# The output gate of the recurrence loaded into the slot of the squares, ahead of the variance sums

## The chip, the core and the metric

The kernel runs on one core of one Trainium2 chip. A core has five engines with an instruction queue each: TensorE (PE, with its weight loads shown as PEld), VectorE (DVE), ScalarE (ACT), GpSimd (POOL) and SyncE (SP). An engine works through its own queue in order and waits at an instruction whose operands or whose memory slot is not free yet. Most DMA transfers are issued from SP's queue, some from POOL's. The metric is the device time of one execution in microseconds (us); the median of three runs is given.

## The reference

The reference is one block of a network: two token mixers side by side (a softmax attention with forgetting, "fox", and a linear recurrence, "rwkv7"), and a feed-forward part behind them. The sequence has 1024 tokens, the model 1024 columns, each mixer 8 heads of 64. The change touches only the end of the recurrence, the normalisation of each head's output and the output gate:

```python
_, y = lax.scan(step, state0, (...))
mean = jnp.mean(y, axis=-1, keepdims=True)
var = jnp.mean(jnp.square(y - mean), axis=-1, keepdims=True)
y = ((y - mean) * lax.rsqrt(var + GN_EPS)).reshape(bsz, seq, RWKV_WIDTH) * ln_w + ln_b
bonus = (jnp.sum(r_h * k_h * r_k, axis=-1, keepdims=True) * v_h).reshape(bsz, seq, RWKV_WIDTH)
return ((y + bonus) * g).astype(p.dtype)
```

Here g is the output gate, `sigmoid(xg) @ g2`, which does not depend on the recurrence.

## The kernel before, in words

The kernel is one program in stages: modulation and normalisation of the input; low-rank products for decay, learning rate and output gate, written to a DRAM tensor d_lora; the recurrence; the attention heads; the output projections; the feed-forward part.

The recurrence works on transposed data: 128 rows are two heads of 64, 512 columns are half of the sequence. That gives eight units, p = 0..3 (pairs of heads) times hf = 0, 1 (halves of the sequence), in this order. Each unit is a coroutine `pre` (preparation: cumulative decay sums cum at L715, exponentials el and en at L719 and L721, the products of the chunks, and the inverse of a triangular matrix by steps on DVE, L784 and L786, with tiles E, t and M) and a coroutine `main` (the copies X and TT of the inverse at L852 and L859, products uw and mz, the chain of states S at L903, and the end of the unit). `pre` of the next unit runs beside `main` of this one. Between their steps PE gets matmuls of the big projections, which need no recurrence: queries and keys (qk), the recurrence's own inputs (ps_rkv), values (v) and gates (gt). A small planner, class Weave, writes this mixture by estimated times. It fixes PE's order. The order of DVE, ACT, POOL and SP in this stage is laid out by the framework when the program is built: by the planned readiness of each instruction, so a change of one wait can move its neighbours.

The end of a unit, L914 to L938, works on tiles of 128x512 in slots of one buffer each, named by their tag. y is the recurrence's output. `head_sums` (L690) adds up each head's 64 rows with a matmul against a block matrix blk_r, in two parts, high and low: ACT casts the high part (L692), POOL subtracts to get the low part (L693), and PE multiplies both. The first call gives the mean (tile mu), which is subtracted at L923. The squares ysq (L925, slot "ysq") go through head_sums a second time, with the parts in the slots "Zt" and "Wt", and give the variance va. rs is the norm factor, exp(-0.5 ln(var + eps)), by two ACT steps (L930, L931), in the slot "ysq". Two DVE steps (L932, L933) scale y and add the bias and the bonus. The gate gg is loaded by SP (L935) into the slot "Zt", the product o is made at L937 in the slot "ysq", and stored to DRAM (L938).

Two neighbours matter at the eighth unit's end. Gate projections run beside it: a half of 24 matmuls goes to one of two PSUM buffers ("big"), ACT takes three steps (L337 to L339) in an SBUF tile gs, DVE one (L340), which reads the PSUM buffer last, ACT one more (L341), and SP stores it (L342, d_gate<-gs). gs has two buffers, so a third half waits until the first one's store has landed. From the attention stage on, gate projections go to the tile rk_ps in the PSUM buffer that has come free, with L1163 and L1164 as the ACT steps that read it. And the loads of the first attention head, stA, stB and vh (L996 to L1000, some 2 MB), are issued from POOL's queue, right behind the low part of the last squares.

## Time and profile before

| what | value |
| --- | --- |
| median of three runs | 1667.04 us (1666.05 to 1668.51) |
| the profiled execution | 1660.79 us, of it span 1659.0 us |
| PE busy | 1613.1 us (97%) |
| DVE busy | 1223.7 us (74%) |
| ACT busy | 822.6 us (50%) |
| POOL busy | 128.9 us (8%) |
| DMA traffic | 240.59 MB, mean 145 GB/s |
| recurrence, from the first gate load to the last product | about 277 to 622 us of the span |

The profile is that of one execution, taken by the hardware profiler. "Idle before" in a row is the time for which the engine had nothing to do before that instruction, with what ended it, found from the semaphores. The chain of waits follows the work back from the last instruction, at each step to what released it. Rows of a timeline give the start in us from the span's start, the duration in us, the engine, the line, the operation, its output and inputs, the number of merged instructions, and in brackets the idle time.

### The profile page before, as it was taken

What the parts mean: (1) busy time and instruction counts of PE and PEld (TensorE: products, weight loads), DVE (VectorE), ACT (ScalarE), POOL (GpSimd) and SP (SyncE); (2) the same over time, 40 slices, a digit from 0 to 9 for tenths busy, and PEclk for the clock granted to TensorE, in tenths of its full rate; (3) what the DMA queues carried; (4) which work ended last, traced back from release to release, by engine and by line L of the source; (5) the groups of instructions that cost most, each with busy time, mean ns of one, the idle gap of its engine ahead of it and who ended that gap; (6) DMA issues with size and microseconds to landing.
All of it is one profiled execution on the core that took longest, in us unless ns stands there. A gap on an engine that the chain in (4) does not pass through costs nothing.

```text
span 1659.0 us, 25949 instructions
## 1 busy us (share of the span) xinstructions
PE 1613.1 (97%) x9694; PEld 1343.8 (81%) x9694; DVE 1223.7 (74%) x2371; ACT 822.6 (50%) x1540; POOL 128.9 (8%) x152
## 2 busy tenths in 40 slices
PE   8999999999999999999999999999999999999998
PEld 7777778787978778888778887888888888888886
DVE  5786787878876526888678447897777777786677
ACT  5563335445455646766623225654444444555455
POOL 0011101111111010221022000000000000000000
PEclk9999999999999999999999999999999999999999
DMA  9488645443333345433187411233223223574363
GB/s 337 136 325 237 178 117 141 134 121 94 112 107 92 96 133 145 128 110 115 57 322 269 170 74 54 68 136 108 96 95 121 96 97 107 209 266 154 125 210 108
DMA packets 121645, 240.59 MB, mean 145 GB/s; under 512 B 40048, under 2 KB 48880, under 8 KB 121520
## 3 DMA queue, kind: packets, MB, share of 16 engines
q1 hardware_dynamic: 113040, 220.58, 40.8%
q0 software_dynamic: 8480, 18.37, 4.2%
q8 instruction: 76, 1.25, 0.3%
q14 instruction: 49, 0.40, 0.1%
HBM read 173.35 MB, written 65.54 MB: 144 GB/s over the span
## 4 chain that ended last, share of the span: by engine, by line
PE 61%; DVE 4%; DMA 1%; ACT 1%; issue 1%; SPq 0%; DVEq 0%; ACTq 0%
PE X L141 14%; PE D L141 13%; PE Y L141 7%; PE wo L141 5%; PE br L141 5%; PE rk_ps L141 4%; PE gt L141 3%; PE W L141 3%; PE lg L141 2%; PE ov L141 2%; PE tp L145 2%; DMA gg<-d_lora 1%; DVE nm L1050 1%; DVE P L1060 1%; DMA g<-d_gate 0%
## 5 line engine op out<-in xcount | busy, mean ns | idle before, releaser
L141 PE MATMUL D<-op,op 128*128 128x512 f32 x924 | 209.8, 389 | 0.0
L141 PEld LDWEIGHTS D<-op,op 128*128 128x128 f32 x924 | 173.4, 188 | 36.2 <-DVE op L1253 0.3
L141 PE MATMUL X<-T_m,S 128*128 128x512 f32 x440 | 106.9, 389 | 0.0
L141 PEld LDWEIGHTS X<-T_m,S 128*128 128x128 f32 x440 | 82.5, 188 | 17.6 <-ACT x L1543 0.4
L1252 ACT CAST op<-g 128x512 fp32r<-128x512 f32 x77 | 47.8, 621 | 73.5 <-PE D L141 48.3
L1253 DVE TENSOR_TENSOR op<-g,op 128x512 fp32r<-128x512 f32 x77 | 53.0, 689 | 41.2 <-ACT op L1252 41.2
L1503 DVE SCALAR_TENSOR_TENSOR c<-ab,vec,c 128x512 f32<-128x512 f32 x88 | 65.9, 750 | 18.4 <-ACT c L1506 16.9
L784 DVE TENSOR_TENSOR t<-E,M 128x60 f32<-128x60 f32 (+24 forms) x248 | 57.7, 233 | 24.7 <-DMA M<-sm 18.8
L274 DVE TENSOR_TENSOR lo_in<-raw_in,hi_in 128x512 fp32r<-128x512 f32 x84 | 57.8, 726 | 20.9 <-PE gt L141 7.2
L1467 DVE TENSOR_TENSOR A<-ur,A 128x512 fp32r<-128x512 f32 x64 | 44.0, 688 | 39.0 <-ACT A L1463 38.8
L1467 DVE TENSOR_TENSOR S<-ur,S 128x512 fp32r<-128x512 f32 x66 | 45.5, 691 | 35.3 <-ACT S L1463 35.1
L1463 ACT CAST S<-ur 128x512 fp32r<-128x512 f32 x66 | 41.0, 622 | 55.9 <-DVE ur L1456 30.9
L141 PE MATMUL Y<-T_h,S 128*128 128x512 f32 x264 | 65.6, 398 | 1.6 <-ACT T_h L1721 1.0
L141 PE MATMUL Y<-T_h,A 128*128 128x512 f32 x264 | 63.4, 389 | 0.0
L1054 ACT ACTIVATE P<-lg,nm 128x896 f32<-128x896 f32 (+3 forms) x64 | 47.5, 744 | 29.0 <-DVE nm L1050 20.8
L141 PEld LDWEIGHTS Y<-T_h,S 128*128 128x128 f32 x264 | 50.6, 192 | 13.4 <-ACT T_h L1721 1.7
L1463 ACT CAST A<-ur 128x512 fp32r<-128x512 f32 x64 | 39.6, 621 | 42.7 <-PE X L141 29.2
L786 DVE TENSOR_TENSOR E<-E,t 128x60 f32<-128x60 f32 (+24 forms) x248 | 55.9, 225 | 6.6
L141 PE MATMUL W<-B_f,A 128*128 128x512 f32 x252 | 60.6, 389 | 0.0
L141 PE MATMUL X<-B_b,A 128*128 128x512 f32 x252 | 60.5, 389 | 0.0
L141 PEld LDWEIGHTS Y<-T_h,A 128*128 128x128 f32 x264 | 49.5, 188 | 10.3
L272 ACT CAST hi_in<-raw_in 128x1024 fp32r<-128x1024 f32 x42 | 43.8, 1048 | 24.6 <-PE ps_rkv L141 9.4
(481 smaller groups left out, 4135.6 us busy)
## 6 DMA issues: line engine op xcount, KB each, us to landing
raw_in<-in_w_in SPq DMA_DIRECT2D x50, 512.0 KB, 3.8
wm<-in_w_mod SPq DMA_DIRECT2D x48, 512.0 KB, 6.7
ur<-in_w_up SPq DMA_DIRECT2D x44, 512.0 KB, 4.1
g<-d_g SPq DMA_DIRECT2D x35, 512.0 KB, 3.9
d_g<-gs SPq DMA_DIRECT2D x44, 256.0 KB, 2.0
d_g<-c SPq DMA_DIRECT2D x33, 256.0 KB, 4.4
d_st<-qh SPq DMA_DIRECT2D x64, 128.0 KB, 2.5
stA<-d_st POOLq DMA_DIRECT2D x8, 1024.0 KB, 6.5
```

The costliest lines, as they stand in the source:

```text
L141: nc.tensor.matmul(o, lhsT, rhs, start=start, stop=stop, skip_group_check=more)
L145: nc.tensor.transpose(o, i, eye)
L272: nc.scalar.copy(hi, raw)
L274: nc.vector.tensor_tensor(lo[:, c : c + NH], raw[:, c : c + NH], f32(hi[:, c : c + NH]), op=ALU.subtract)
L784: tt(tv, E32[:, 0:J, s : s + 1].to_broadcast([128, J, W]), M32[:, s : s + 1, s + 1 : 32].to_broadcast([128, J, W]), op=ALU.mult)
L786: tt(E32[:, 0:J, s + 1 : 32], E32[:, 0:J, s + 1 : 32], tv, op=ALU.add)
L1054: nc.scalar.activation(e[:, 0:n], lg[:, 0:n], AF.Exp, bias=nm[:, 0:1], accum_out=nm[:, 1:2])
L1252: nc.scalar.copy(hi, src)
L1253: tt(lo, src, f32(hi), op=ALU.subtract)
L1463: nc.scalar.copy(hi, src)
L1467: tt(lo, src, f32(hi), op=ALU.subtract)
L1503: stt(c, ab[:, x + hf * NH : x + hf * NH + NH], V("conv_w", 22 * x + i), c, op0=ALU.mult, op1=ALU.add)
```

## The change

The load of the gate moves from behind the second scaling step to the place right behind the second head_sums, and from the slot "Zt" to the slot "ysq", whose squares have been read by then. The norm factor rs takes the slot "Zt". The product is made in place, in gg, so that the extra tile o falls away, and the store reads gg.

```diff
             yield from head_sums(va, ysq, part("Zt", "s"), part("Wt", "s"))
-            rs = rw.tile([128, NH], F32, tag="ysq", name=f"rs{n}", bufs=1)
+            gg = rw.tile([128, NH], F32, tag="ysq", name=f"gg{n}", bufs=1)
+            nc.sync.dma_start(gg, d_lora[2, p, :, cs])
+            rs = rw.tile([128, NH], F32, tag="Zt", name=f"rs{n}", bufs=1)
             nc.scalar.activation(rs, va, AF.Ln, scale=1.0 / CH, bias=epsr[:, 1:2])
             nc.scalar.activation(rs, rs, AF.Exp, scale=-0.5)
             stt(y, y, V("ln_w", p), rs, op0=ALU.mult, op1=ALU.mult)
             stt(y, y, V("ln_b", p), bon, op0=ALU.add, op1=ALU.add)
-            gg = rw.tile([128, NH], F32, tag="Zt", name=f"gg{n}", bufs=1)
-            nc.sync.dma_start(gg, d_lora[2, p, :, cs])
-            ov = rw.tile([128, NH], F32, tag="ysq", name=f"o{n}", bufs=1)
-            tt(ov, y, gg, op=ALU.mult)
-            nc.sync.dma_start(d_orw[p, :, cs], ov)
+            tt(gg, y, gg, op=ALU.mult)
+            nc.sync.dma_start(d_orw[p, :, cs], gg)
```

In the built program PE's and POOL's orders are the same as before. On SP the load gg goes ahead of the stores of queries in the first unit, ahead of the loads M in the fourth, and ahead of one gate store or one weight load in the seventh and eighth. On DVE the sums cum of the next unit go ahead of other steps by one to three places in the first, second, third and fifth unit; on ACT the exponentials el and en go ahead of the copies TT in the first and fifth unit and ahead of a weight cast in the third.

## The prediction

> **What bounds the kernel now.** I read the page first, then the chain of waits, the tiles that the change touches, and the timelines around the places the chain names.

> ```profile
> span 1659.0 us, 25949 instructions
> ...
> PE 1613.1 (97%) x9694; PEld 1343.8 (81%) x9694; DVE 1223.7 (74%) x2371; ACT 822.6 (50%) x1540; POOL 128.9 (8%) x152
> ```

> TensorE (PE) is busy 97% of the span, so a change to a VectorE tail of the recurrence can only matter where PE waits for it. The profiled execution took 1660.79 us, 1659.0 of it span; the median of the runs shown is 1667.04. I work out a difference in the profiled execution and add it to the median. The gate load gg does stand in the chain of waits, at the last of the eight units:

> ```profile
> 610.67 10.26 DMA gg<-d_lora
> ...
> 621.66 0.70 DVE gs L340
> ...
> 622.39 7.37 PE rk_ps L141 x24
> ```

> ```profile
> DMA to landing us min/median/max: 3.0/3.4/10.3
> ```

> The load normally lands 3.0 to 3.4 us after its issue; the last took 10.3. In the chain the DVE gate evacuation gs follows it, then the matmuls of rk_ps. Here is that place engine by engine (PE, ACT, POOL, DVE, SP; start, duration, in brackets the idle time before and its releaser):

> ```profile
> 617.03 1.98 PE L141 MATMUL gt<-u_hi,lo_in 128*128 128x512 f32 x8
> 622.39 2.92 PE L141 MATMUL rk_ps<-u_hi,hi_in 128*128 128x512 f32 x8 [3.39 <-DVE gs L340]
> ...
> 630.93 1.43 PE L141 MATMUL rk_ps<-u_hi,hi_in 128*128 128x512 f32 x5 [1.17 <-ACT gm L1164]
> ```

> ```profile
> 614.89 0.63 ACT L339 ACTIVATE gs<-gs 128x512 f32<-128x512 f32 x1
> ...
> 625.74 0.60 ACT L337 ACTIVATE gs<-gt 128x512 f32<-128x512 f32 x1 [2.73 <-DMA d_gate<-gs]
> ...
> 629.79 0.60 ACT L1163 ACTIVATE gs<-rk_ps 128x512 f32<-128x512 f32 x1 [0.74 <-PE rk_ps L141]
> ```

> ```profile
> 606.36 1.30 POOL L693 TENSOR_TENSOR Wts<-ysq,Zts 128x512 fp32r<-128x512 f32 x1 [5.08 <-ACT Zts L692]
> 607.60 0.73 POOL L996 DMA_DIRECT2D stA<-d_st  x1
> ```

> ```profile
> 613.06 0.75 DVE L933 SCALAR_TENSOR_TENSOR y<-y,vec,bon 128x512 f32<-128x512 f32 x1
> 621.05 0.69 DVE L937 TENSOR_TENSOR o<-y,gg 128x512 f32<-128x512 f32 x1 [7.23 <-DMA gg<-d_lora]
> ```

> ```profile
> 610.67 0.32 SPq L935 DMA_DIRECT2D gg<-d_lora  x1
> 611.04 0.42 SPq L342 DMA_DIRECT2D d_gate<-gs  x1
> ```

> ```profile
> 624.00:628.00 4.00, 4.00 (x13) 3.10 (x12) 0.30 (x1) 1.86 (x3) 0.00 (x0) 0.64 1.27 235
> ```

> The DVE product o could have run at 613.8; it waited until 621.05, held the evacuation behind it on DVE's queue, and PE stood 3.39 us. The granted clock then was 0.64 in 624 to 628: 24 matmuls of rk_ps took 7.37 us. At full clock eight take 1.82 (the distance of two starts, 0.227 each), so 24 take 5.45. A second stall of 1.17 follows.

> **The change at the last unit.** It removes nothing from the amount of work: the same loads, products and stores, one tile fewer. Earlier gg waited for its slot (Zt) until the second variance matmul; now it waits only until POOL has read the squares, at 606.36 + 1.30 = 607.66. In the built program it also moves ahead of the weight load raw_in on SP. So its issue moves from 610.67 to about 607.7, and the large head load stA, issued at 607.60 on POOL, is no longer ahead of it by 3 us. With the 3.0 to 3.4 us of the other loads it lands at 610.7 to 611.1; if stA's megabyte gets in first, at most 10.3 us after issue, 618. I take 611, as its issue now almost coincides with stA's. Then o runs at 613.8, and the evacuation at 615.6 (ACT's L339 ends at 615.52), and PE goes on at 618.9 without the 3.39 us.

> What is late next? ACT reaches its next gate step, L337, at 616.9, but its tile is free only when the store of the gate issued at 611.04 has landed: that is the wait of 2.73 us that ended at 625.74. The evacuation of the first rk_ps half (L1163, L1164) stands behind that gate on ACT's queue, and the second half's matmuls wait for it. Their start is L337's start plus (630.93 − 625.74) = 5.19, less the 0.74 us by which ACT was idle before L1163: plus 4.45. If the store lands no earlier, PE resumes at 630.2, only 0.74 sooner. But in the queue the gate's store takes the place that gg had, and gg landed at 620.9 there. So I take L337 at 621.5 (bounds: 616.9, ACT's own time, and 625.74). PE then resumes at 626.0 instead of 630.93, a gain of 4.9 us. At an L337 of 621.1 or sooner the first half itself decides: 618.9 + 5.45 = 624.4, plus the 1.14 from L1163 to the matmuls: 625.5, a gain of 5.4, the most there is. Everything after hangs on this chain.

> [...]

> **The other units.** There gg is not waited for, so its earlier landing is worth nothing (PE and DVE have other work). What costs is the order: DVE and ACT are ordered by the planner, which now believes that SP is free earlier and puts the next unit's cumulative sums (L715) and exponentials (el, en, L719 and L721) sooner. In the built program this happens in the first, third and fifth unit. PE's order is unchanged.

> First unit: SP's order loses gg ahead of cum, and both sums move ahead of lo_in on DVE, both exponentials ahead of the copies TT on ACT.

> ```profile
> 277.65 0.52 SPq L935 DMA_DIRECT2D gg<-d_lora  x1
> 278.29 1.38 SPq L711 DMA_DIRECT2D cum<-d_lora  x1
> ```

> ```profile
> DMA to landing us min/median/max: 2.7/3.0/3.3
> ```

> ```profile
> 279.64 0.23 DVE L784 TENSOR_TENSOR t<-E,M 128x76 f32<-128x76 f32 x1
> ...
> 282.50 1.27 DVE L715 TENSOR_TENSOR_SCAN cum<-cst,cum 128x256 f32<-128x256 f32 x2
> ```

> ```profile
> 279.80 0.75 ACT L859 COPY TT<-zi 32x256 f32<-32x256 f32 x2 [1.05 <-PE zi L141]
> ...
> 283.81 0.63 ACT L719 ACTIVATE el<-cum 128x512 f32<-128x512 f32 x1 [2.20 <-DVE cum L715]
> 284.35 0.62 ACT L721 ACTIVATE en<-cum 128x512 f32<-128x512 f32 x1
> 284.87 0.62 ACT L730 ACTIVATE ksq<-ksq 128x512 f32<-128x512 f32 x1
> ```

> ```profile
> 282.18 1.96 PE L141 MATMUL uw<-QA,TT 64*64 64x128 f32 x32
> ...
> 298.46 0.43 PE L141 MATMUL sp<-S,Mt 128*128 128x64 f32 x2 [1.49 <-ACT S L903]
> ```

> cum is issued at 277.65, 0.64 sooner, and lands 2.7 to 3.3 us later (the bracket of L711): I take 3.3, 280.95, since in this place it came later, 282.5 at most, which with 0.64 off gives the upper bound 281.85. DVE is there at 279.87 and has been dense since: it now stands 1.1 us (0.5 to 2.0). el starts 1.31 after the sums (282.50 to 283.81), at 282.26; en and the next ACT step follow at 0.54 and 0.52, so TT runs at 283.32 to 284.08 instead of 279.80 to 280.56. The matmuls uw need TT and start at 284.1 instead of 282.18: PE stands 1.95 us. At 298.46 PE had waited 1.49 us for S, which follows DVE's queue; that absorbs 1.49 of the 1.95, but S itself comes 1.1 later. So this unit costs the larger, **1.1 us** (0.5 to 2.0).

> Fifth unit: the same move.

> ```profile
> 476.89 0.63 ACT L339 ACTIVATE gs<-gs 128x512 f32<-128x512 f32 x1
> 477.43 0.73 ACT L859 COPY TT<-zi 32x256 f32<-32x256 f32 x2
> ```

> ```profile
> 473.21 0.38 SPq L711 DMA_DIRECT2D cum<-d_lora  x1
> ```

> ```profile
> 478.73 1.96 PE L141 MATMUL uw<-QA,TT 64*64 64x128 f32 x32
> ```

> cum lands at 473.21 + 3.0 = 476.2; el starts at 477.5, en at 478.06, L339 at 478.58, TT at 479.12 instead of 477.43, ready at 479.85. uw starts at 479.9 instead of 478.73: **1.2 us** (0.9 with a landing of 2.7, 1.5 with 3.3). No later stall of PE on DVE is there to absorb it.

> Third unit: both sums follow each other and el comes sooner; a weight cast (hi_in, 1.05 us) goes behind en.

> ```profile
> 378.85 0.63 ACT L719 ACTIVATE el<-cum 128x512 f32<-128x512 f32 x1 [1.12 <-DVE cum L715]
> ```

> ```profile
> 375.65 0.75 DVE L933 SCALAR_TENSOR_TENSOR y<-y,vec,bon 128x512 f32<-128x512 f32 x1
> ...
> 378.14 0.68 DVE L715 TENSOR_TENSOR_SCAN cum<-cst,cum 128x256 f32<-128x256 f32 x1
> ```

> ```profile
> 380.44 2.35 PE L141 MATMUL uw<-QA,TT 64*64 64x128 f32 x32 [0.69 <-ACT TT L859]
> ```

> Both halves of the sum now run in the place of y's second step, from 375.65 on, instead of ending with the half at 378.14; so el moves from 378.85 to 375.65 + 1.31 = 377.0. en, the cast and TT follow at 0.54, 0.52 and about 1.05, so TT starts at 379.1 and ends by 379.9. PE's 0.69 us before uw goes: **−0.7 us** (−0.7 to 0).

> Fourth unit: gg moves ahead of four loads M on SP, and would hold them if POOL were late.

> ```profile
> 414.72 1.30 POOL L693 TENSOR_TENSOR Wts<-ysq,Zts 128x512 fp32r<-128x512 f32 x1 [0.20 <-ACT Zts L692]
> ```

> ```profile
> 419.02 1.83 SPq L776 DMA_DIRECT2D M<-sm  x2
> ```

> POOL is done at 416.02, the loads issue at 419.02: nothing. In the second, sixth, seventh and eighth units SP and DVE change places by a step or none; cover is PE's queue of projection matmuls, and without it each would cost at most the 0.2 us of one step. Zt is freed sooner (by rs's reader, not by o): gains nothing, since Zt's next writer comes a unit later.

> Sum: −4.9 + 1.1 + 1.2 − 0.7 = −3.3 us, so 1667.04 − 3.3 = **1663.7 us**. 0.2% is 3.3 us, about what a measurement of this kernel can tell from no change; the forecast sits on that edge.

> **Rivals.**
> 1. The gate's store does not come sooner (the end bound of L337, 625.74). For it: the store took 14.7 us, and the head load runs through all of that time whatever gg does. Against: gg, one place ahead in the same queue, landed 4.8 us earlier. PE resumes 0.74 sooner but has stood 618.9+5.45=624.4 to 630.2, and after 3.39 us of standing the clock cost 7.37 − 5.45 = 1.9; paying it again here, where the old payment is saved in the first half but not used, gives −0.74 + 1.9 = +1.2. Sum: 1.2 + 1.1 + 1.2 − 0.7 = +2.8: 1669.8, slower than before. It decides from L337 at about 624 on, where the gain falls below the 1.6 us that the other units cost. With the first unit at 2.0 it is 1670.7.
> 2. The exponentials cost nothing: cum lands early or PE's later stalls absorb the delay. For it: 1.49 us was absorbable in the first unit. Against: DVE's rows there show no idle time. −4.9 − 0.7 = −5.6: 1661.4.
> 3. The 1.95 us stand in the first unit slows PE's clock, as the 3.39 us stand did. Then 1.95 + 1.9 − 1.49 = 2.4 instead of 1.1: sum −2.0, 1665.0.
> That the change does not do what it says (gg behind stA) leads into rival 1: the load lands up to 618 and the rest follows the store.

> **How the numbers follow.** Forecast 0.42 (its own range 1661.5 to 1665.5, from the bounds of its terms; half of it beyond −0.2%), rival 1 0.25, rival 2 0.18, rival 3 0.15. Faster by over 0.2%: 0.21 + 0.18 = 0.39, put at 0.40. Slower by over 0.2%: most of rival 1 when its other terms sit at their upper bounds, 0.18. Within: 0.42. The range 1660.0 to 1670.7 reaches from rival 2 with the largest gain (−0.5 more, and the first unit's gap gone) to rival 1's upper value.

> **What would show it.** gg of the last unit issued near 607.7 by the new span's own clock and landing within 4 us; no DVE wait on gg; L337's wait on d_gate ended some 4 us sooner; rk_ps without a 3.39 us stand and no window at 0.64. In the first and fifth unit a PE wait for ACT's TT ahead of uw of 2 and 1.2 us; in the third that wait gone. The prediction is wrong if L337's wait keeps its end, if the waits before uw are absent, or if a stall of the half-clock kind appears elsewhere.

## The result, and the profile after

| kernel | median | runs | from, to |
| --- | --- | --- | --- |
| before | 1663.19 us | 12 | 1659.19 to 1668.51 |
| after | 1659.54 us | 12 | 1656.04 to 1662.12 |

The ratio is 0.9977, with a 95% interval of 0.9966 to 0.9988: the change makes the kernel 0.23% faster. The medians lie 3.65 us apart, where 3.3 us had been forecast; the interval reaches from 2.0 to 5.7 us. The ratios here and below are the recorded ones, and need not be the quotient of the two medians. The absolute time lies outside the range given (1660.0 to 1670.7), since the kernel before came out at 1663.19 over twelve runs and not at the 1667.04 of the three that were shown.

The page of the profile after, first lines. The profiled execution took 1662.01 us:

```profile
span 1660.2 us, 25947 instructions
...
PE 1615.2 (97%) x9694; PEld 1346.1 (81%) x9694; DVE 1223.2 (74%) x2371; ACT 822.3 (50%) x1540; POOL 130.3 (8%) x152
```

This execution is 1.2 us longer than the one profiled before, although the median is 3.65 us shorter. So the two profiles are read place by place, not by their totals. Here is the chain of waits in order of time at the end of the eighth unit (start, us, what), followed by the group of the gate loads:

```profile
613.93 0.46 PE va L141 x2
614.39 8.18 PE gt L141 x36
622.56 5.45 PE rk_ps L141 x24
...
628.04 0.60 ACT gs L1162
628.64 0.50 ACT gm L1163
...
629.18 4.61 PE rk_ps L141 x19
```

```profile
L930 SPq DMA_DIRECT2D gg<-d_lora x8: 319/338/431, 271.1 to 611.2; - x8
...
DMA to landing us min/median/max: 2.0/2.7/3.7
```

The gate load and the DVE gate evacuation gs are gone from the chain: PE's gate projection (gt) leads straight to the 24 matmuls of rk_ps. The last load is issued at 611.25. The landing line counts loads and the stores that read the tile, where it has a landing for them: four loads, of 2.6 to 3.7 us, where the longest was 10.3. The last load is not among them; its 128 packets of 2 KB in the trace ended at 613.69, 2.44 us after issue, and the product that reads it ran at 617.46 without a wait. Next comes the same place engine by engine (PE, ACT, DVE, SP, then a window with its granted clock after the busy times); all its times are 3.6 us later than in the profile before, because of what the earlier units cost in this execution:

```profile
622.40 1.98 PE L141 MATMUL rk_ps<-u_hi,hi_in 128*128 128x512 f32 x8
...
629.18 2.11 PE L141 MATMUL rk_ps<-u_hi,hi_in 128*128 128x512 f32 x8 [1.18 <-ACT gm L1163]
...
623.34 0.60 ACT L337 ACTIVATE gs<-gt 128x512 f32<-128x512 f32 x1 [2.86 <-DMA d_gate<-gs]
...
628.04 0.60 ACT L1162 ACTIVATE gs<-rk_ps 128x512 f32<-128x512 f32 x1 [1.39 <-PE rk_ps L141]
...
617.46 0.69 DVE L936 TENSOR_TENSOR gg<-y,gg 128x512 f32<-128x512 f32 x1
...
611.25 0.32 SPq L930 DMA_DIRECT2D gg<-d_lora  x1
...
614.59 0.32 SPq L342 DMA_DIRECT2D d_gate<-gs  x1
...
624.00:628.00 4.00, 4.00 (x18) 2.99 (x16) 0.69 (x1) 1.86 (x3) 0.06 (x1) 1.00 1.26 293
```

PE's stand of 3.39 us before rk_ps is gone, and the granted clock in 624 to 628 is 1.00 instead of 0.64; the next slow stretch in this trace starts at 682. The gate store issued at 614.59 is waited for until 623.34, which is 8.75 us after issue. Before, it was 14.7 (611.04 to 625.74). The second stand, for ACT's gm, is the same as before: 1.18 us.

What each place cost can be read from the start of PE's instructions: the same matmul in both traces, and how the distance between the two changes across a place. The table gives this for after and for the experiments of the next section (us, plus is a loss). Places with no edit near them show the scatter of this reading, about 0.4 us, but 1.1 us at the eighth unit's end in all_but_last.

| kernel | first unit (230 to 303) | third (376 to 384) | fifth (475 to 485) | eighth's end (560 to 675) |
| --- | --- | --- | --- | --- |
| after | +2.2 | -0.4 | +1.3 | -5.3 |
| last_only | +0.1 | -0.3 | 0.0 | -5.3 |
| all_but_last | +1.3 | -0.8 | +1.4 | -1.1 |
| third_last | +0.1 | -1.1 | 0.0 | -5.3 |
| after_held | +1.5 | -1.0 | 0.0 | -5.3 |
| after_ordered | +0.4 | -0.7 | 0.0 | -5.3 |
| no_gate_last | -0.2 | +0.4 | -0.2 | -5.3 |
| product_behind | -0.2 | -0.2 | 0.0 | +2.6 |

The first unit in the profile after (DVE, ACT, PE, and a window with its clock), the fifth (ACT, PE) and the third (PE):

```profile
281.77 1.27 DVE L715 TENSOR_TENSOR_SCAN cum<-cst,cum 128x256 f32<-128x256 f32 x2 [1.67 <-DMA cum<-d_lora]
...
283.08 0.63 ACT L719 ACTIVATE el<-cum 128x512 f32<-128x512 f32 x1 [4.00 <-DVE cum L715]
...
284.14 0.73 ACT L859 COPY TT<-zi 32x256 f32<-32x256 f32 x2
...
284.54 2.96 PE L141 MATMUL uw<-QA,TT 64*64 64x128 f32 x32 [2.05 <-ACT TT L859]
...
286.00:290.00 4.00, 4.00 (x23) 3.19 (x18) 3.82 (x14) 1.71 (x5) 0.61 (x2) 0.57 0.71 238
```

```profile
479.69 0.64 ACT L719 ACTIVATE el<-cum 128x512 f32<-128x512 f32 x1 [0.86 <-DVE cum L715]
...
481.27 0.73 ACT L859 COPY TT<-zi 32x256 f32<-32x256 f32 x2
...
481.67 2.35 PE L141 MATMUL uw<-QA,TT 64*64 64x128 f32 x32 [0.89 <-ACT TT L859]
```

```profile
382.44 1.80 PE L141 MATMUL uw<-QA,TT 64*64 64x128 f32 x24
```

In the first unit DVE stands 1.67 us for the load of cum, both exponentials go ahead of TT on ACT, and PE stands 2.05 us before uw. Behind that stand the clock was granted at 0.57 in 286 to 290; the place costs 2.2 us. In the fifth unit PE stands 0.89 us before uw and the place costs 1.3 us. In the third the wait of 0.69 us before uw is gone. The four places make -2.2 us, or -3.1 with the 1.3 that the first unit costs in all_but_last, where no slow clock follows its stand. That the profiled execution is 1.2 longer all the same is due mostly to two more stretches of half clock, at 682 and at 935 us, that its execution had and the one before had not in this length: +1.6 us at each. The last section says what is known of them.

### The profile page after: what moved, and what is told of

The parts are those of the page before. It is cut to its first block, busy times and chain, and to the rows that moved or that the text cites. A ratio compares the mean times of both kernels' runs of the same rounds, so it can differ in the third digit from the quotient of the medians.

```text
span 1660.2 us, 25947 instructions
## 1 busy us (share of the span) xinstructions
PE 1615.2 (97%) x9694; PEld 1346.1 (81%) x9694; DVE 1223.2 (74%) x2371; ACT 822.3 (50%) x1540; POOL 130.3 (8%) x152
## 4 chain that ended last, share of the span: by engine, by line
PE 62%; DVE 3%; ACT 2%; DMA 1%; issue 1%; SPq 0%; ACTq 0%; DVEq 0%
PE X L141 14%; PE D L141 13%; PE Y L141 7%; PE wo L141 5%; PE br L141 5%; PE gt L141 4%; PE rk_ps L141 4%; PE W L141 3%; PE lg L141 2%; PE ov L141 2%; PE tp L145 2%; DVE nm L1049 1%; DVE P L1059 1%; DMA g<-d_gate 0%; DVE tl L1089 0%
## 5 line engine op out<-in xcount | busy, mean ns | idle before, releaser
L141 PE MATMUL D<-op,op 128*128 128x512 f32 x924 | 209.8, 389 | 0.0
L141 PEld LDWEIGHTS D<-op,op 128*128 128x128 f32 x924 | 173.3, 188 | 36.3 <-DVE op L1252 0.3
L141 PE MATMUL X<-T_m,S 128*128 128x512 f32 x440 | 106.9, 389 | 0.0
L141 PEld LDWEIGHTS X<-T_m,S 128*128 128x128 f32 x440 | 82.5, 188 | 17.5 <-ACT x L1542 0.4
L784 DVE TENSOR_TENSOR t<-E,M 128x60 f32<-128x60 f32 (+24 forms) x248 | 56.1, 226 | 26.6 <-DMA M<-sm 20.6
L141 PE MATMUL Y<-T_h,S 128*128 128x512 f32 x264 | 65.6, 398 | 1.6 <-ACT T_h L1720 1.0
L141 PE MATMUL Y<-T_h,A 128*128 128x512 f32 x264 | 63.4, 389 | 0.0
L141 PEld LDWEIGHTS Y<-T_h,S 128*128 128x128 f32 x264 | 50.6, 192 | 13.4 <-ACT T_h L1720 1.8
L141 PE MATMUL W<-B_f,A 128*128 128x512 f32 x252 | 60.6, 389 | 0.0
L141 PE MATMUL X<-B_b,A 128*128 128x512 f32 x252 | 60.5, 389 | 0.0
L141 PEld LDWEIGHTS Y<-T_h,A 128*128 128x128 f32 x264 | 49.5, 188 | 10.3
```

What stands on the lines that cost most here:

```text
L141: nc.tensor.matmul(o, lhsT, rhs, start=start, stop=stop, skip_group_check=more)
L784: tt(tv, E32[:, 0:J, s : s + 1].to_broadcast([128, J, W]), M32[:, s : s + 1, s + 1 : 32].to_broadcast([128, J, W]), op=ALU.mult)
```

## The experiments

The theory: the gain is made at the eighth unit's end alone, where two waits go together; the loss is made in the first and the fifth unit by the new order of DVE's and ACT's steps, not by the loads themselves. Rivals: the gain needs the early load elsewhere too, or is chance; the gate's store waits for the head load whatever SP issues ahead of it; the wait of the product is the whole loss.

**The change in one unit, in all the others, and in the two that gained.** Three kernels choose the units in which the gate is loaded early (load_gate issues the load):

```diff
+            early = (p, hf) in [(3, 1)]
+            a_tag, b_tag = ("ysq", "Zt") if early else ("Zt", "ysq")
...
+            if early:
+                gg = load_gate()
+            rs = rw.tile([128, NH], F32, tag=b_tag, name=f"rs{n}", bufs=1)
```

The list is (3, 1) for last_only, the other seven units for all_but_last, and (1, 0) and (3, 1) for third_last.

> The gate is loaded early in the eighth unit alone; the other seven load it as before, and only one load changes its place, on SP, ahead of the weight load raw_in. My theory (the gain is the last unit's, the losses come from the planner's new order in the first and fifth unit): the stand of 3.39 us before rk_ps goes, L337's wait for the gate store ends near 619.8 instead of 625.74, no PE wait before uw in the first and fifth unit beyond those of before, the 0.69 us one in the third stays; 5.4 us faster than before (ratio 0.9968). Rival A (the early load in the other units matters too, so the parts are not separable): the last unit's gain is smaller than 4 us here, ratio above 0.9976. Rival B (the difference measured between the two kernels is chance windows of half clock, not the last unit): ratio 0.999 to 1.001.

Measured: 1657.19 us (6 runs) against 1662.74 of the kernel before (23 runs beside it), 5.55 us faster, ratio 0.9963 (0.9949 to 0.9976). ACT and PE at that place (before these starts the kernel had lost 2.9 us at places that were not edited):

```profile
622.93 0.60 ACT L337 ACTIVATE gs<-gt 128x512 f32<-128x512 f32 x1 [3.17 <-DMA d_gate<-gs]
...
621.69 1.98 PE L141 MATMUL rk_ps<-u_hi,hi_in 128*128 128x512 f32 x8
...
628.47 2.11 PE L141 MATMUL rk_ps<-u_hi,hi_in 128*128 128x512 f32 x8 [1.18 <-ACT gm L1174]
```

L337's wait ends at 622.93, 620.1 on the time scale of the profile before, and rk_ps starts with no stand. Rival B is out, and so is rival A by the trace (-5.3 here and in after).

> The gate is loaded early in the first seven units, and late as before in the eighth. My theory: the eighth unit keeps its stand of 3.39 us and its L337 wait to about 625.7; the first unit's uw waits 2.05 us for TT, the fifth's 0.89 us, the third's wait is gone; 1.6 us slower than before (ratio 1.0010) without a half clock window behind the first unit's stand, 2.9 us (1.0017) with one. Rival (the exponentials ahead of TT cost nothing, the later stalls absorb them): 0.7 us faster, ratio 0.9996.

Measured: 1664.44 us (12 runs), 1.70 us slower than before, ratio 1.0008 (0.9995 to 1.0021). The interval excludes neither the rival's 0.9996 nor no change at all; the trace speaks for the theory. PE in the first unit, the window behind it with its clock, and PE at the eighth unit's end:

```profile
284.34 2.35 PE L141 MATMUL uw<-QA,TT 64*64 64x128 f32 x32 [1.88 <-ACT TT L859]
...
286.00:290.00 4.00, 4.00 (x26) 3.00 (x22) 3.79 (x15) 1.84 (x6) 0.61 (x2) 1.00 0.66 215
...
623.62 2.75 PE L141 MATMUL rk_ps<-u_hi,hi_in 128*128 128x512 f32 x8 [2.28 <-DVE gs L340]
```

The waits before uw are there (1.88 us here, 0.92 in the fifth unit), the stand of the eighth unit stays (2.28 us here for 3.39, at a place without an edit; hence the -1.1 of the table), and the first unit costs 1.3 us. The two halves add up: -5.55 + 1.70 = -3.85, beside the -3.65 of the whole change, within intervals of some 2 us each way. The stand of 1.88 us is almost that of the kernel after, yet the clock behind it is 1.00 in 286 to 290 instead of 0.57; the last section comes back to that.

> The gate is loaded early in the third and the eighth unit alone, the two that gained. My theory: the last unit gains 5.4 us and the third 0.6 (its PE wait of 0.69 us before uw is gone), with no loss elsewhere: 6.0 us faster than before (ratio 0.9964), 2.4 us faster than the full change. Rival (the third unit's wait is taken up by a later one, so that nothing is left of it at the end): the same as the early load in the eighth unit alone, 5.4 us, ratio 0.9968.

Measured: 1656.65 us (6 runs), 6.09 us faster than before, ratio 0.9956 (0.9940 to 0.9972). This is the lowest median found. Each against its own runs of the kernel before, it wins 2.4 us more than the full change, though the two intervals overlap, and it cannot be told from last_only. The interval cannot tell 6.0 from 5.4; in the trace the third unit's wait before uw is gone, and of the 1.1 us won there 1.0 are left at 541 us. Since the same reading scatters by 0.4, the third unit's share is likely and not certain.

**The orders put back.** In after_held the exponentials stay behind the copies TT on ACT, by an order without a semaphore; in after_ordered the sums stay behind y's second step on DVE as well:

```diff
+        def hold(k):
+            if ("en", k) in marks and ("TT", k - 2) in marks:
+                for x in ("el", "en"):
+                    tc.add_manual_dep(marks[x, k].ins, marks["TT", k - 2].ins.name, NOSYNC)
+
+        def hold_sums(k):
+            if ("en", k) in marks and ("o", k - 3) in marks:
+                for c0 in (0, 256):
+                    tc.add_manual_dep(marks["cum", k, c0].ins, marks["o", k - 3].ins.name, NOSYNC)
```

Here marks["o", k] is the second scaling step (the line with ln_b), k counts the units from 0, and hold is called for k = 3 and 7: what moves ahead in the first and fifth unit belongs to the unit two later than that of the copies TT. The sums and exponentials in question are thus those of the unit three after the one that ends (k = 3 where k = 0 ends), and not of the next one, as the description of the change has it.

> The full change, with one order on ACT put back: the exponentials el and en of the unit two later stay behind the copies TT in the first and the fifth unit. The sums cum stay moved ahead on DVE, as in the full change. My theory (ACT's order makes the waits before uw): these waits go (at most 0.3 us left of 2.05 and 0.89), and of the order on DVE at most 0.8 us of delay is left in the first unit's S; 5 to 6 us faster than before (ratio 0.9964 to 0.9970). Rival (DVE's stand for the sums, not ACT's order, is what costs): the first unit still loses 1 to 2 us at the wait of sp for S, and the kernel is 3.5 to 4.5 us faster than before, about as the full change (ratio 0.9973 to 0.9979).

Measured: 1659.01 us (12 runs), 3.73 us faster than before, ratio 0.9976 (0.9966 to 0.9986). The rival's number. ACT, DVE and PE in the first unit:

```profile
280.28 0.75 ACT L866 COPY TT<-zi 32x256 f32<-32x256 f32 x2 [0.96 <-PE zi L141]
...
282.05 1.27 DVE L720 TENSOR_TENSOR_SCAN cum<-cst,cum 128x256 f32<-128x256 f32 x2 [1.69 <-DMA cum<-d_lora]
...
289.02 1.96 PE L141 MATMUL mz<-E,Wt 64*64 64x128 f32 x32 [0.95 <-DVE t L791]
...
300.48 0.43 PE L141 MATMUL sp<-S,Mt 128*128 128x64 f32 x2 [2.01 <-ACT S L912]
```

TT is early again and uw has no wait. But DVE's stand of 1.69 us is as it was, and it surfaces behind uw: PE waits 0.95 us for DVE before mz at 289.02 and then 2.01 us for S instead of 1.49. The first unit still loses 1.5 us. My expectation of at most 0.8 was wrong: it took the delay of DVE as absorbed. In the fifth unit DVE stands for cum too, 0.72 us here, but nothing of it reaches PE: ACT's order was the whole loss, which fell from 1.3 to 0.

> The full change, with the orders on DVE and on ACT put back in the first and the fifth unit: the sums cum of the unit two later stay behind the second scaling step of y on DVE, the exponentials behind the copies TT on ACT. The loads gg stay early in all eight units. My theory (the two orders together make the loss of the first unit, either of them alone is enough for it, since DVE's stand of 1.67 us for cum ends in S later and ACT's order in TT later): DVE has no stand for cum there, uw waits 0.3 us at most, sp's wait for S is 1.5 us as before, and the kernel is 6.0 us faster than before (ratio 0.9964), like the early load in the third and eighth unit alone. Rival (the loads' new places on SP, or the shifts in the other units, cost too): as with ACT's order alone put back, 3.7 us (0.9976).

Measured: 1657.49 us (5 runs), 5.25 us faster than before, ratio 0.9966 (0.9954 to 0.9978). DVE and PE:

```profile
281.07 1.27 DVE L725 TENSOR_TENSOR_SCAN cum<-cst,cum 128x256 f32<-128x256 f32 x2
...
297.72 0.43 PE L141 MATMUL sp<-S,Mt 128*128 128x64 f32 x2 [0.94 <-ACT S L918]
```

cum runs without a stand, uw has no wait, and PE's wait for S is 0.94 us. All eight gate loads are early in this kernel, so their new places on SP cost nothing that this reading can show. The median sits between the two forecasts, 0.75 us from one and 1.5 from the other, and the interval reaches both; it is the trace, with 0.4 and 0.0 us lost in the first and fifth unit, that speaks for the theory.

**The eighth unit's end.** no_gate_last takes gg's load out of the queue there and so leaves out the output gate in that unit; product_behind exchanges two steps on DVE:

```diff
-            nc.sync.dma_start(gg, d_lora[2, p, :, cs])
+            if (p, hf) != (3, 1):
+                nc.sync.dma_start(gg, d_lora[2, p, :, cs])
...
-            tt(ov, y, gg, op=ALU.mult)
+            tt(ov, y, y if (p, hf) == (3, 1) else gg, op=ALU.mult)
```

```diff
-            stt(g, ps, 0.0, g, op0=ALU.min, op1=ALU.subtract)
+            low = stt(g, ps, 0.0, g, op0=ALU.min, op1=ALU.subtract)
+            if "o" in marks:
+                tc.add_manual_dep(marks.pop("o").ins, low.ins.name, NOSYNC)
...
-            tt(ov, y, gg, op=ALU.mult)
+            prod = tt(ov, y, gg, op=ALU.mult)
+            if (p, hf) == (3, 1):
+                marks["o"] = prod
```

> The kernel before, with the gate of the eighth unit not loaded at all: its product is y times y, so in that unit the output gate is left out. The gate store of the projection beside it is then the next transfer of SP's queue in gg's place, issued at about 610.7, and the head load is untouched. My theory (gg, 256 KB right ahead of it on the same queue, held the store): the store lands some 6 us sooner, L337's wait for it ends at 619.8 or sooner, rk_ps has no stand of 3.39 us, 5.4 us faster than before (ratio 0.9968). Rival (the store waits for the head load's earlier writes, whatever stands ahead of it on SP): L337 still at 625.7, PE stands about 5.8 us before the second half of rk_ps, 0.7 us faster to 1.2 us slower than before (ratio 0.9996 to 1.0007).

Measured: 1657.12 us (7 runs) against 1662.74 (18 runs beside it), 5.62 us faster, ratio 0.9964 (0.9950 to 0.9978). SP, ACT and PE:

```profile
611.98 0.32 SPq L342 DMA_DIRECT2D d_gate<-gs  x1
...
620.99 0.60 ACT L337 ACTIVATE gs<-gt 128x512 f32<-128x512 f32 x1 [3.13 <-DMA d_gate<-gs]
...
619.79 1.98 PE L141 MATMUL rk_ps<-u_hi,hi_in 128*128 128x512 f32 x8
...
626.56 2.11 PE L141 MATMUL rk_ps<-u_hi,hi_in 128*128 128x512 f32 x8 [1.18 <-ACT gm L1165]
```

The store, issued at 611.98, has landed by 620.99: 9.0 us instead of 14.7, with the head load as before. So gg close ahead of it in the queue was what held it for the rest. In the profile after, gg is ahead of the store too, but by 3.3 us, and its packets have ended before the store is issued; there the store takes 8.75 us, about as long as without gg.

> The kernel before, with one exchange on DVE: the eighth unit's product o goes behind the gate evacuation L340 that it held up. The load gg stays late, ahead of the gate store on SP. My theory (two waits stand one behind the other, the product's for gg and L337's for the gate store, and both need gg early): the stand of 3.39 us goes, but L337 still starts at 625.7, PE stands 5.8 us before the second half of rk_ps (resumes 0.74 us sooner than before) and pays a half clock behind it: 0.7 us faster to 1.2 us slower than before (ratio 0.9996 to 1.0007). Rival (the product's wait on DVE was the whole loss): 4 us faster or more, ratio 0.9976 or below.

Measured: 1662.98 us (12 runs), 0.24 us slower than before, ratio 1.0001 (0.9989 to 1.0014). DVE, ACT and PE:

```profile
616.81 0.69 DVE L340 SCALAR_TENSOR_TENSOR gs<-gt,gs 128x512 f32<-128x512 f32 x1 [1.74 <-ACT gs L339]
622.62 0.69 DVE L939 TENSOR_TENSOR o<-y,gg 128x512 f32<-128x512 f32 x1 [5.12 <-DMA gg<-d_lora]
...
627.87 0.60 ACT L337 ACTIVATE gs<-gt 128x512 f32<-128x512 f32 x1 [9.70 <-DMA d_gate<-gs]
...
620.10 1.98 PE L141 MATMUL rk_ps<-u_hi,hi_in 128*128 128x512 f32 x8
...
632.20 3.78 PE L141 MATMUL rk_ps<-u_hi,hi_in 128*128 128x512 f32 x8 [6.51 <-ACT gm L1168]
```

The exchange does what it says: the evacuation runs at 616.81, and rk_ps starts at 620.10 without a stand. But L337 waits for the gate store to 627.87 and PE stands 6.51 us before the second half. Freeing DVE alone wins nothing; the early load frees DVE and the store together.

## Why the prediction was right or wrong

- **The absolute time** is the step that failed: "I work out a difference in the profiled execution and add it to the median". That median was of three runs, 1667.04. The text named the profiled execution's 1660.79, 6.25 us lower, and left the gap unexplained. Twelve runs gave 1663.19, and 1663.19 - 3.3 would have been 1659.9. The range took its width from the four places and nothing for the base; moved by the base's 3.85 us it would have been 1656.2 to 1666.9, with the result inside. The spread goes with the granted clock: of 23 later runs of the kernel before, the five with a mean clock of 0.995 took 1659.17 to 1662.80 us, the four with 0.989 or less 1665.41 to 1668.35.
- **The low ends of the ranges** do not come out of the terms. Rival 2's 1661.4 less the 0.5 makes 1660.9, and what is left to 1660.0 has no figure. The bounds of the four terms lead to 1662.3, and not 1661.5, for the forecast's own range.
- **The difference** came out at 3.65 for 3.3, which is closer than its parts: the eighth unit won 0.4 more than forecast and the first cost 0.2 to 1.1 more, and the two errors cancel in part. That is luck.
- **The eighth unit**: -5.3 measured for -4.9. Right in both waits and in their order. L337 was taken at 621.5 and came at 619.7 on the time scale of the profile before (623.34 - 3.6), so the first half of rk_ps decides, the case that the text gave as "a gain of 5.4, the most there is". gg's packets ended 2.44 us after issue, which fits the landing that was said. The "3.0 to 3.4" of the other loads rested on two loads, the only others with a landing in that profile. What had made gg late is less clear than the text has it: stA itself landed at 613.39, 7.5 us ahead of gg. The 128 packets of 4 KB of the weight load raw_in, which SP issued at 609.11 ahead of gg, ran until 616.89, and stB landed at 625.92. The early load goes ahead of raw_in and stB and is issued level with stA, and no run separates them.
- **The first unit**: 1.1 forecast (0.5 to 2.0), 1.3 without a slowed clock and 2.2 with it (rival 3 had 2.4). The stand before uw was 2.05 for 1.95. The load of cum took 3.9 us (277.87 to 281.77) and not 3.3, so DVE stood 1.67 us and not 1.1. That the larger of two delays counts was right: putting back ACT's order alone left a loss of 1.5. DVE's order alone was not put back.
- **Rival 3**, the clock behind that stand, happened in the profile of after (0.57) and not in that of all_but_last (1.00). It is neither a fixed cost nor absent.
- **The fifth unit**: 1.3 for 1.2. The wait before uw was 0.89, and zi ahead of it waited 0.51 for ACT, where it had waited 0.24 before. **The third**: -0.4 to -1.1 for -0.7; the kernels without an edit there show -0.3 to +0.4.
- **Rival 1** is refuted by no_gate_last and last_only: the store came 5.7 us sooner with the head load unchanged. What the 9.0 us that are left go back to, the head load or the 512 KB of raw_in right ahead of the store on SP, was not shown; no run here took either away. The store did not wait for the whole head load: in the profile after it has landed by 623.34, and stB and vh, issued ahead of it at 611.89 and 612.89, landed at 627.34 and 629.60. In the profile before, the trace shows the store's data moved by 622.13, and L337's wait for it ended at 625.74. Two 4-byte packets of SP's DMA queue that end in between took 1.40 and 2.01 us, where most take 0.01 to 0.03, the last until 624.33. Whether they belong to this store, and what they waited for, was not shown.
- **Rival 2** is refuted by all_but_last: the exponentials and sums cost 1.3 and 1.4 us in the first and the fifth unit, and both losses go where the two orders are put back.

## What to carry to other kernels

When a wait is taken away, ask which transfer takes its place in the queue: here a store stood behind the load and came 5.7 us sooner without it, and freeing the engine alone was worth nothing. An edit that moves one load can reorder other engines where a planner lays out the order; making the change only in the two units that gained won 6.09 us for 3.65, though the two intervals overlap. And a base of three runs is no base for an effect of 0.2%: predict the difference, and ask what makes the runs differ before adding it to a time.
